# Branch B's key, value and query operands: split into halves at their source, and stored in DRAM as halves

## The chip, the cores and the metric

The kernel runs on one core of one Trainium2 chip. The metric is device time in microseconds (us) of one execution. A core has a matrix engine (TensorE, PE in the profile; its weight loads are shown as PEld), a vector engine (DVE), a scalar engine (ACT), GpSimd (POOL) and SyncE (SP). In this kernel SP issues every DMA; sixteen DMA engines carry them out.

## The reference

Two layers (DEPTH 2) of one mixer each run over 1024 latent tokens and 256 context tokens, 1280 in all, with D_MODEL 1024. Three branches work on the same normalised input: A is windowed grouped-query attention, B is multi-head latent attention, C is a gated convolution. Each branch is gated, projected and merged. Only branch B matters for the change. Cut to that:

```python
def mla_project(q_lat, kv_lat, g_qa, w_qb, g_kva, w_kvb):
    q = (rms_norm(q_lat, g_qa) @ w_qb).reshape(B, T, H_B, NOPE_B + ROPE_B)
    kv = (rms_norm(kv_lat, g_kva) @ w_kvb).reshape(B, T, H_B, NOPE_B + V_B)
    return q[..., :NOPE_B], q[..., NOPE_B:], kv[..., :NOPE_B], kv[..., NOPE_B:]

def block(qs):
    q_n, q_r = qs
    s = (jnp.einsum('bqhd,bkhd->bhqk', q_n, keys_n)
         + jnp.einsum('bqhd,bkd->bhqk', q_r, keys_r))
    p = jax.nn.softmax(s.astype(jnp.float32) * SCALE_B, axis=-1)
    return jnp.einsum('bhqk,bkhd->bqhd', p.astype(vals.dtype), vals)
```

There are 8 heads. `keys_n` is per head, `keys_r` (the rotary key) is shared by the heads. Latent queries read all 1280 keys; context queries read the 256 context keys, and are computed in layer 0 only, since the last layer's context output is not used.

## The kernel before

**Halves.** All matrix products are made in fp32r, a float32 that TensorE reads at its fast rate with fewer bits. To keep the accuracy, an operand x is split into a high half, hi = x rounded to fp32r, and a low half, lo = x - hi. `hi_act` (L104) makes hi on ACT, `lo_dve` (L110) makes lo on DVE. A product is then three passes, hi hi, hi lo and lo hi. In the profile the lines of these helpers, L105 and L111, stand for every split in the kernel; the tile's name tells which.

**Order of a layer.** `run` (L1594) goes through: input projection; token-major projections and branch C; then the preparation of the attentions: `a_prepare` (L892) and `b_keys` (L944), run alternately; `b_queries` (L1039); attention A (`attn_a`); attention B (`attn_b`, L1350) with branch A's merge as a filler; the second merge; the output projection.

**b_keys** writes three things to DRAM, as float32. The rotary key `krs` (64 rows by 1280 tokens) is transposed into PSUM, copied by DVE (L977) to a tile and stored. The keys `kns`, four tiles of 128 rows (two heads each), are projected by chunks of 512, 512 and 256 tokens, copied by DVE (L989) and stored. The values `vs`, ten tiles of 128 tokens by 512 columns, are projected, copied by ACT (L1005) and stored. The tiles share one ring of five 2 KB buffers, "kn". Between these steps `other()` runs one step of A's query preparation (tile "qq", ring of 4, stored to `qas`) or of the transposition of the q latents.

**b_queries** makes a head's queries chunk by chunk: nine matmuls, then one DVE multiplication by the rotation factors (L1054), then a store to `qs`. The factors are loaded for every head and chunk (L1046), although they depend only on the chunk and on whether the head is even. In layer 0 this is a stage of its own, 24 blocks. In layer 1 it has 16 blocks, which fill TensorE's gaps in attention A.

**attn_b** reads them back. Per head, `load_k` (three calls, one for each chunk) loads 64 rows of `kns` and 64 rows of `krs` into a staging tile and splits it into the K tile, `load_v` (two calls) does the same for V, and `load_q` for each unit of four query tiles. The staging tile has the tag "f", a ring of F_BUFS = 5 buffers, and the merge that runs beside it takes its own operands g and a from the same ring (L1472, L1473):

```python
f = stage()
nc.sync.dma_start(f[no : no + 64, :n], self.kns[h // 2][no : no + 64, o : o + n])
nc.sync.dma_start(f[ro : ro + 64, :n], self.krs[:, o : o + n])
halves(*(k_()[:, i, o : o + n] for i in range(2)), f[:, :n])
```

**Order inside attention.** `pipeline` (L1065) gives every piece of work (scores, maxima, exponentials, transposes, products with V, loads, filler) a due time on one axis, in estimated us of TensorE, and emits the pieces sorted by it. A unit is four query tiles of one head (and one of two context tiles in layer 0). A preparation of a unit is due at the unit's score start plus an offset: KP0 = -16 for the first K chunk and KP1 = 2 more for each further one, VP0 = 2 for V, QP0 = -5 for Q. K and V have two tiles each, Q three. Each engine runs its instructions in the order in which it got them, and SP issues its DMAs in order, waiting at each for its buffer.

## Time and profile before

| What | us |
| --- | --- |
| median of 3 runs | 3128.86 (3127.94 to 3136.29) |
| the profiled execution | 3132.84 |
| its span in the trace | 3131.1 |
| key preparation, layer 0 and layer 1 | about 925 to 969 and 2465 to 2504 |
| queries of B as a stage, layer 0 | about 969 to 1009 |
| attention A, layer 0 and layer 1 | about 1009 to 1212 and 2504 to 2665 |
| attention B, layer 0 and layer 1 | about 1209 to 1562 and 2664 to 2987 |

The times in the trace are us from the start of the span. The windows view gives, for a stretch, the busy time of each engine with its count of instructions, the clock that TensorE was granted (1.00 is full), the DMA engines' mean busy share and the GB/s that they moved. The view by lines gives for each group the busy time, the mean of one in ns, and the idle time of the engine just before it with what ended it.

### The profile page before, as it was taken

To read this page: it belongs to the slowest core of one execution; us is meant where nothing else is said; L and a number is where in the kernel's file an instruction comes from. 1 tells how busy PE (TensorE), PEld (TensorE's weight loads), DVE (VectorE), ACT (ScalarE), POOL (GpSimd) and SP (SyncE) were. 2 spreads that over 40 slices of the span, in tenths; PEclk is the share of its full clock that TensorE was granted. 3 is DMA by queue.
4 is the path that set the end of the run, shared out by engine and by line. 5 is a ranking of instruction groups with operands and counts; after the bars stand their busy time and mean duration, and the time that the engine had idled before them with its cause. 6 is when DMAs were issued, how large, how long until landed. Compare 5 with 4: busy or idle time off the path is not lost.

```text
span 3131.1 us, 54154 instructions
## 1 busy us (share of the span) xinstructions
PE 3001.9 (96%) x19731; PEld 2690.7 (86%) x19731; DVE 1879.6 (60%) x3213; ACT 1380.6 (44%) x3068; POOL 1413.2 (45%) x1809
## 2 busy tenths in 40 slices
PE   7899999989899999999999989999899999999998
PEld 4899999988897666777789889999889988778888
DVE  4744444444345766699854755555453577689863
ACT  3323333322222665478733423333322366568832
POOL 4545332332130666466652645444241367555641
PEclk9999999999999999999999989999999999999999
DMA  6122232245319434532063322333344442641153
GB/s 217 57 71 68 87 107 95 98 147 161 114 63 306 152 120 131 156 89 56 23 213 108 111 78 82 100 108 106 128 147 127 152 134 75 192 119 50 44 184 108
DMA packets 316227, 366.66 MB, mean 117 GB/s; under 512 B 51126, under 2 KB 242616, under 8 KB 315704
## 3 DMA queue, kind: packets, MB, share of 16 engines
q1 hardware_dynamic: 315960, 363.20, 36.3%
q8 instruction: 155, 2.54, 0.3%
q14 instruction: 112, 0.92, 0.1%
HBM read 256.02 MB, written 107.10 MB: 116 GB/s over the span
## 4 chain that ended last, share of the span: by engine, by line
PE 77%; DVE 7%; DMA 5%; issue 5%; ACT 4%; POOL 2%; SPq 0%; POOLq 0%; ACTq 0%; DVEq 0%
PE T L489 10%; PE T L488 10%; PE T L487 10%; PE T L115 8%; PE T L116 8%; PE T L117 8%; PE O L1198 6%; PE T L1185 5%; PE S L1414 4%; PE S L1283 2%; PE C L217 2%; ACT p L1160 1%; DVE ptL L111 1%; DVE tt L424 1%; DMA raw<-in_w_branch_dram 1%
## 5 line engine op out<-in xcount | busy, mean ns | idle before, releaser
L489 PE MATMUL T<-T,sl 128*128 128x320 f32 (+1 forms) x1408 | 416.5, 296 | 4.9 <-DVE sl L111 4.9
L115 PE MATMUL T<-wh,hm 128*128 128x288 f32 (+1 forms) x1328 | 385.7, 294 | 33.5 <-ACT wh L105 33.5
L487 PE MATMUL T<-T,sh 128*128 128x320 f32 (+1 forms) x1408 | 416.2, 296 | 0.6 <-ACT sh L105 0.6
L488 PE MATMUL T<-T,sh 128*128 128x320 f32 (+1 forms) x1408 | 416.1, 296 | 0.0
L116 PE MATMUL T<-wl,hm 128*128 128x288 f32 (+1 forms) x1328 | 387.2, 292 | 1.5 <-DVE wl L111 1.5
L117 PE MATMUL T<-wh,hm 128*128 128x288 f32 (+1 forms) x1328 | 388.6, 293 | 0.0
L111 DVE TENSOR_TENSOR ptL<-T,ptH 128x512 fp32r<-128x512 f32 (+2 forms) x512 | 335.3, 661 | 73.6 <-ACT ptH L105 70.1
L105 ACT ACTIVATE ptH<-T 128x512 fp32r<-128x512 f32 (+2 forms) x512 | 292.7, 577 | 155.6 <-PE T L1185 133.7
L487 PE MATMUL T<-hm,sh 128*128 128x320 f32 (+1 forms) x1056 | 313.4, 297 | 15.7 <-ACT sh L105 15.7
L493 DVE TENSOR_TENSOR px<-T,px 128x320 f32<-128x320 f32 (+1 forms) x440 | 194.9, 452 | 205.6 <-PE T L489 196.4
L489 PE MATMUL T<-hm,sl 128*128 128x320 f32 (+1 forms) x1056 | 313.0, 296 | 0.0
L488 PE MATMUL T<-hm,sh 128*128 128x320 f32 (+1 forms) x1056 | 312.9, 296 | 0.0
L1185 PE MATMUL T<-ident,p 128*128 128x128 f32 x1888 | 293.0, 275 | 13.0 <-DVE ptL L111 6.1
L1149 DVE TENSOR_REDUCE st<-S 128x1 f32<-128x1024 f32 (+2 forms) x288 | 269.9, 938 | 45.9 <-PE S L1414 19.0
L447 POOL TENSOR_TENSOR ssum<-sraw 128x512 f32<-128x512 f32 x88 | 114.5, 1301 | 395.3 <-DMA sraw<-in_w_in_dram 338.8
L1170 POOL TENSOR_SCALAR p<-p,st 128x1280 f32<-128x1280 f32 (+2 forms) x256 | 279.0, 1090 | 23.6
L115 PEld LDWEIGHTS T<-wh,hm 128*128 128x128 f32 x1328 | 254.2, 193 | 35.4 <-ACT wh L105 35.3
L1185 PEld LDWEIGHTS T<-ident,p 128*128 128x128 f32 x1888 | 221.9, 140 | 72.9 <-DVE ptL L111 21.5
L1160 ACT ACTIVATE p<-S,st 128x1024 f32<-128x1024 f32 (+2 forms) x256 | 241.0, 941 | 83.1 <-DVE st L1149 66.5
L489 PEld LDWEIGHTS T<-T,sl 128*128 128x128 f32 x1408 | 266.4, 189 | 5.4 <-DVE sl L111 5.4
L111 DVE TENSOR_TENSOR sl<-ssum,sh 128x512 fp32r<-128x512 f32 x176 | 163.6, 934 | 174.8 <-ACT sh L105 171.4
L487 PEld LDWEIGHTS T<-T,sh 128*128 128x128 f32 x1408 | 266.3, 189 | 0.8 <-ACT sh L105 0.8
(235 smaller groups left out, 7662.1 us busy)
## 6 DMA issues: line engine op xcount, KB each, us to landing
sraw<-in_w_in_dram SPq DMA_DIRECT2D x28, 1024.0 KB
wm<-in_w_mod_dram SPq DMA_DIRECT2D x24, 1024.0 KB
raw<-in_w_branch_dram SPq DMA_DIRECT2D x36, 512.0 KB
sraw<-in_w_in_dram SPq DMA_DIRECT2D x32, 512.0 KB
g<-sg SPq DMA_DIRECT2D x64, 256.0 KB
a<-macc SPq DMA_DIRECT2D x64, 256.0 KB
raw<-in_w_o_dram SPq DMA_DIRECT2D x14, 1024.0 KB
raw<-in_w_in_dram SPq DMA_DIRECT2D x10, 1024.0 KB
```

Source lines behind the costliest of these rows:

```text
L105: self.nc.scalar.activation(hi, src, AF.Copy)
L111: self.nc.vector.tensor_tensor(lo, src, hi.bitcast(F32), ALU.subtract)
L115: mm(out, lhsT=lh, rhs=rh, start=start, stop=False)
L116: mm(out, lhsT=lh, rhs=rl, start=False, stop=False)
L117: mm(out, lhsT=ll, rhs=rh, start=False, stop=stop)
L487: mm(out, lhsT=hi[:, k], rhs=tH, start=first and k == 0, stop=False, skip_group_check=True)
L488: mm(out, lhsT=hi[:, k], rhs=tL, start=False, stop=False, skip_group_check=True)
L489: mm(out, lhsT=lo[:, k], rhs=tH, start=False, stop=k == half - 1, skip_group_check=True)
L1149: nc.vector.reduce_max(st[:, 0:1], s, axis=AX.X, negate=True)
L1160: nc.scalar.activation(ptile(o, o + ap.shape[-1]), ap, AF.Exp, bias=st[:, len(parts) - 1 : len(parts)], accum_out=st[:, 2 + i : 3 + i])
L1170: nc.gpsimd.tensor_scalar(p, p, st[:, 4:5], 1.0, op0=ALU.mult, op1=ALU.mult)
L1185: nc.tensor.transpose(pt[:, w : w + P], blk, self.ident)
```

## The change

- `b_keys` splits at the source: a new helper `send` takes a result from PSUM, makes hi on ACT and lo on DVE side by side in one tile, and stores both with one DMA. The values are treated alike. The ring "kn" has three buffers of twice the size; the ring "qq" has three for four.
- `krs`, `kns`, `vs` and `qs` in DRAM get a dimension of two for the halves.
- `b_queries` loads the factors once for each chunk and head parity, and runs the chunks in the outer loop and the heads in the inner one. In layer 0 (`self.nq == NT`) it splits the queries and stores two halves; in layer 1 it stores them whole, in the first half.
- `attn_b` loads K as one piece and V as one piece, halves and all, straight into their tiles; in layer 0 also Q. In layer 1 Q is still split there. KP1 is gone, VP0 is 0.

```diff
-KP0, KP1, VP0, QP0 = -16.0, 2.0, 2.0, -5.0
+KP0, VP0, QP0 = -16.0, 0.0, -5.0
...
+        def both():
+            return kp.tile([P, 2, 512], F32R, tag="kn", name=self.nm("kn"), bufs=3)
+
+        def send(dst, rows, o, n, pt):
+            x = both()[:rows, :, :n]
+            self.hi_act(x[:, 0], pt[:rows, :n])
+            self.lo_dve(x[:, 1], pt[:rows, :n], x[:, 0])
+            nc.sync.dma_start(dst[:, :, o : o + n].rearrange("i p t -> p i t"), x.bitcast(F32))
...
-            kr = kp.tile([P, 512], F32, tag="kn", name=self.nm("kr"), bufs=5)
-            nc.vector.tensor_copy(kr[:64, :n], pt[:64, :n])
-            nc.sync.dma_start(self.krs[:, o : o + n], kr[:64, :n])
+            send(self.krs, 64, o, n, pt)
...
-                kn = kp.tile([P, 512], F32, tag="kn", name=self.nm("kn"), bufs=5)
-                nc.vector.tensor_copy(kn[:, :n], pt)
-                nc.sync.dma_start(self.kns[p][:, o : o + n], kn[:, :n])
+                send(self.kns[p], P, o, n, pt)
...
-            vv = kp.tile([P, H * HD], F32, tag="kn", name=self.nm("vv"), bufs=5)
-            nc.scalar.activation(vv, pt, AF.Copy)
-            nc.sync.dma_start(self.vs[:, t], vv)
+            vv = both()
+            self.hi_act(vv[:, 0], pt)
+            self.lo_dve(vv[:, 1], pt, vv[:, 0])
+            nc.sync.dma_start(self.vs[:, t], vv.bitcast(F32))
...
-            nc.sync.dma_start(self.qs[h][:, o : o + n], q[:, :n])
+            if self.nq < NT:
+                nc.sync.dma_start(self.qs[h][0, :, o : o + n], q[:, :n])
+                return
+            hi, lo = (pool.tile([P, 512], F32R, tag=f"qo{i}", name=self.nm("qo"), bufs=3) for i in "HL")
+            self.hi_act(hi[:, :n], q[:, :n])
+            self.lo_dve(lo[:, :n], q[:, :n], hi[:, :n])
+            for i, x in enumerate((hi, lo)):
+                nc.sync.dma_start(self.qs[h][i, :, o : o + n], x[:, :n].bitcast(F32))
...
-        for h in range(H):
-            for c in self.chunks:
-                got = self.lazy(lambda h=h, c=c: load(h, c))
+        for c in self.chunks:
+            tabs = [self.lazy(lambda e=e, c=c: load(e, c)) for e in range(2)]
+            for h in range(H):
+                got = tabs[h % 2]
...
+            def load_k(h=h, no=no, ro=ro, k_=k_):
+                for r, src in ((no, self.kns[h // 2][:, no : no + 64]), (ro, self.krs)):
+                    nc.sync.dma_start(k_()[r : r + 64].bitcast(F32), src.rearrange("i p t -> p i t"))
+
+            def load_v(h=h, v_=v_):
+                for i in range(2):
+                    nc.sync.dma_start(
+                        v_()[:, :, i * HD : (i + 1) * HD].bitcast(F32), self.vs[:, :, i, h * HD : (h + 1) * HD]
+                    )
...
+                if self.nq == NT:
+                    nc.sync.dma_start(q_()[:, :, :n].bitcast(F32), src.rearrange("i p t -> p i t"))
+                    return
...
+            kprep = [(KP0, load_k), (VP0, load_v)]
```

The ring of the factors' tile goes from 6 to 4 buffers in layer 0 and from 2 to 3 in layer 1.

More of the change, by code (lines that the diff above doesn't have):

```diff
@@ L918, in step @@
             for i, (a, b) in enumerate(((0, 64), (64, 0))):
-                q = tp.tile([P, 512], F32R, tag="qq", name=self.nm("qq"), bufs=4)
+                q = tp.tile([P, 512], F32R, tag="qq", name=self.nm("qq"), bufs=3)
                 self.hi_act(q[a : a + 64, :n], pt[a : a + 64, :n])
@@ L1041, in b_queries, with load @@
         nc = self.nc
-        def load(h, c):
+        def load(e, c):
             o, n = CH[c]
             tb = pool.tile([P, 512], F32, tag="tab", name=self.nm("tab"), bufs=bufs)
-            nc.sync.dma_start(tb[:, :n], self.a["k_rope_t"][h % 2][:, o : o + n])
+            nc.sync.dma_start(tb[:, :n], self.a["k_rope_t"][e][:, o : o + n])
             return tb
@@ L1367, in attn_b @@
             v_ = self.lazy(lambda: tp.tile([P, NT, P], F32R, tag="v", name=self.nm("v"), bufs=2))
-            def load_k(c, h=h, no=no, ro=ro, k_=k_):
-                o, n = CH[c]
-                f = stage()
-                nc.sync.dma_start(f[no : no + 64, :n], self.kns[h // 2][no : no + 64, o : o + n])
-                nc.sync.dma_start(f[ro : ro + 64, :n], self.krs[:, o : o + n])
-                halves(*(k_()[:, i, o : o + n] for i in range(2)), f[:, :n])
-            def load_v(c, h=h, v_=v_):
-                t0, nt = c * (NT // 2), NT // 2
-                f = stage()[:, : nt * HD].rearrange("p (t d) -> p t d", d=HD)
-                nc.sync.dma_start(f, self.vs[:, t0 : t0 + nt, h * HD : (h + 1) * HD])
-                halves(*(v_()[:, t0 : t0 + nt, i * HD : (i + 1) * HD] for i in range(2)), f)
+            def load_k(h=h, no=no, ro=ro, k_=k_):
[6 more added lines that the diff above has]
+                    )
             def load_q(q_, t0, t1, h=h):
                 n = (t1 - t0) * P
+                src = self.qs[h][:, :, t0 * P : t1 * P]
+                if self.nq == NT:
+                    nc.sync.dma_start(q_()[:, :, :n].bitcast(F32), src.rearrange("i p t -> p i t"))
+                    return
                 f = stage()
-                nc.sync.dma_start(f[:, :n], self.qs[h][:, t0 * P : t1 * P])
+                nc.sync.dma_start(f[:, :n], src[0])
                 halves(*(q_()[:, i, :n] for i in range(2)), f[:, :n])
-            kprep = [(KP0 + i * KP1, lambda c=c, load_k=load_k: load_k(c)) for i, c in enumerate((0, 1, 2))]
-            kprep += [(VP0 + c * KP1, lambda c=c, load_v=load_v: load_v(c)) for c in range(2)]
+            kprep = [(KP0, load_k), (VP0, load_v)]
             def score(t, t0, q, k_=k_):
@@ L1665, in run @@
             self.bz = [self.dram([P, T], F32, "bz") for _ in range(4)]
-            self.krs = self.dram([64, T], F32, "krs")
-            self.kns = [self.dram([P, T], F32, "kns") for _ in range(4)]
+            self.krs = self.dram([2, 64, T], F32, "krs")
+            self.kns = [self.dram([2, P, T], F32, "kns") for _ in range(4)]
             self.qas = [self.dram([P, T], F32, "qas") for _ in range(H)]
-            self.qs = [self.dram([P, T], F32, "qs") for _ in range(H)]
+            self.qs = [self.dram([2, P, T], F32, "qs") for _ in range(H)]
             self.vas = self.dram([P, NT, 4 * HD], F32, "vas")
-            self.vs = self.dram([P, NT, H * HD], F32, "vs")
+            self.vs = self.dram([P, NT, 2, H * HD], F32, "vs")
             self.in_proj(ew, first, begin, ehp.close)
@@ L1694, in run @@
                 qp = self.pool(el, "qp")
-                steps = self.b_queries(qp, ws, qH, qL, self.bank, 6)
+                steps = self.b_queries(qp, ws, qH, qL, self.bank, 4)
                 for i, (_, _, fn) in enumerate(steps):
@@ L1709, in run @@
             if last:
-                fill = self.b_queries(lp, ws, qH, qL, self.cbank, 2)
+                fill = self.b_queries(lp, ws, qH, qL, self.cbank, 3)
             else:
```

## The prediction

> **What bounds the kernel now.** I read the page's table of engines, then the windows over the stages that the change touches, then lines and timelines inside them. The page first:
>
> ```profile
> span 3131.1 us, 54154 instructions
> PE 3001.9 (96%) x19731; PEld 2690.7 (86%) x19731; DVE 1879.6 (60%) x3213; ACT 1380.6 (44%) x3068; POOL 1413.2 (45%) x1809
> ```
>
> TensorE (PE) is busy 96% of the span, so an edit that takes work from DVE and ACT only pays where one of these makes PE late. The windows (PE, PEld, DVE, ACT, POOL busy, clock, DMA share, GB/s) of the steady part of attention B, a stretch and three heads of layer 0, then three stretches of layer 1:
>
> ```profile
> 1346.00:1378.22 32.22, 29.68 (x169) 22.87 (x169) 31.50 (x55) 26.26 (x62) 22.35 (x29) 1.00 0.40 112
> 1413.40:1449.94 36.54, 35.43 (x206) 28.80 (x207) 33.95 (x60) 30.87 (x70) 28.05 (x38) 1.00 0.23 63
> 1449.94:1485.26 35.32, 34.73 (x206) 28.87 (x206) 32.43 (x60) 30.63 (x70) 19.29 (x29) 1.00 0.18 50
> 1485.26:1521.50 36.24, 35.40 (x206) 28.82 (x206) 34.02 (x60) 30.78 (x70) 27.99 (x38) 1.00 0.15 43
> 2780.00:2800.00 20.00, 19.11 (x110) 15.12 (x109) 19.79 (x35) 16.97 (x38) 15.06 (x18) 1.00 0.45 129
> 2851.36:2883.94 32.58, 32.54 (x193) 27.15 (x193) 30.64 (x54) 28.12 (x62) 22.65 (x31) 1.00 0.23 64
> 2916.20:2948.00 31.80, 31.78 (x187) 26.23 (x186) 28.18 (x49) 25.84 (x56) 22.60 (x30) 1.00 0.12 35
> ```
>
> DVE is nearly full in all of them, and in layer 0 PE has holes beside it (29.68 of 32.22 us in the first row). A head of layer 0 takes 36.0 us (mean of rows two to four); one of layer 1 takes 32.6 us (the 2851 row) with PE closed. So DVE limits layer 0's heads, PE those of layer 1.
>
> The windows of the key preparation and the query projection tell another story:
>
> ```profile
> 925.00:1009.00 84.00, 83.70 (x462) 70.16 (x461) 53.23 (x101) 31.37 (x71) 3.05 (x6) 1.00 0.86 290
> 933.00:941.00 8.00, 8.00 (x52) 6.91 (x51) 7.69 (x18) 2.98 (x6) 0.00 (x0) 1.00 0.63 216
> 957.00:965.00 8.00, 8.00 (x44) 6.50 (x43) 3.73 (x8) 5.63 (x12) 0.00 (x0) 1.00 1.03 375
> 973.00:981.00 8.00, 8.00 (x41) 6.68 (x40) 3.20 (x7) 0.00 (x0) 0.00 (x0) 1.00 1.02 356
> 2465.00:2507.00 42.00, 41.30 (x239) 34.60 (x237) 33.21 (x63) 26.12 (x60) 4.08 (x8) 1.00 0.81 283
> 2497.00:2505.00 8.00, 8.00 (x36) 6.44 (x35) 0.71 (x2) 3.95 (x8) 0.00 (x0) 1.00 0.95 352
> ```
>
> Here PE is closed and the DMA engines are almost full too: a share of 0.86 in layer 0, 0.81 in layer 1, with 375 GB/s the most that a full stretch moved. This is where the change doubles what is written.
>
> **Part 1: the splits leave attention B.** By lines and forms, DVE in layer 0's attention B (1209 to 1562 us), and then in layer 1's (2664 to 2987 us):
>
> ```profile
> L111 DVE TENSOR_TENSOR k<-f,k 128x512 fp32r<-128x512 f32 x16 | 14.3, 898 | 3.9 <-ACT k L105 3.7
> L111 DVE TENSOR_TENSOR q<-f,q 128x512 fp32r<-128x512 f32 x16 | 13.6, 852 | 2.9 <-ACT q L105 2.9
> L111 DVE TENSOR_TENSOR v<-f,v 128x320 fp32r<-128x320 f32 x16 | 10.7, 666 | 0.0
> L111 DVE TENSOR_TENSOR k<-f,k 128x256 fp32r<-128x256 f32 x8 | 4.2, 526 | 6.7 <-ACT k L105 6.7
> L111 DVE TENSOR_TENSOR q<-f,q 128x256 fp32r<-128x256 f32 x8 | 4.1, 508 | 1.0 <-ACT q L105 1.0
> ```
>
> ```profile
> L111 DVE TENSOR_TENSOR k<-f,k 128x512 fp32r<-128x512 f32 x16 | 11.0, 708 | 3.1 <-ACT k L105 3.1
> L111 DVE TENSOR_TENSOR v<-f,v 128x320 fp32r<-128x320 f32 x16 | 10.9, 704 | 0.4 <-ACT v L105 0.4
> L111 DVE TENSOR_TENSOR k<-f,k 128x256 fp32r<-128x256 f32 x8 | 4.6, 569 | 2.4 <-ACT k L105 2.4
> ```
>
> Layer 0 loses 14.3 + 13.6 + 10.7 + 4.2 + 4.1 = 46.9 us of DVE, 5.9 us a head. Layer 1 keeps the split of Q (its queries are still written whole) and loses 26.5 us. What is that worth? In layer 0 a head's DVE falls from 33.5 (mean of the three rows) to 27.6 us, and PE is late next. PE's own need I take from layer 1: 32.6 us, plus the context unit, which layer 1 does not have: per head 10 matmuls of 256 columns and 4 transposes. Their spacing stands in PE's timeline, the 256-column starts 0.12 us apart and ten transposes in 1.26 us:
>
> ```profile
> 1236.11 0.28 PE L116 MATMUL T<-yL,wh 128*128 128x256 f32 x1
> 1236.23 0.28 PE L117 MATMUL T<-yH,wl 128*128 128x256 f32 x1
> ...
> 924.79 1.26 PE L905 MATMUL T<-ident,kA 128*128 128x128 f32 x10
> ```
>
> That is 10 x 0.12 + 4 x 0.11 = 1.6, so 34.2 us a head: 1.8 us saved on each of about five heads (1378 to 1562 us), **-9**. The bounds are 0 (the holes are PE's own order) and -14 (also the DVE-full 1346 row, and every head at 33.5). Layer 1 gives nothing in the steady part: from 2916.20 no next head is split, and PE still needs 31.80/187 = 0.170 us per matmul, against 32.58/193 = 0.169. Only 2780 to 2820 us, where DVE is full while the merge ends, can give its idle time, 0.9 us of the row and about as much behind it: **-1.5**.
>
> **Part 2: the start of attention B.** The staging tile "f" has five buffers, shared with the merge's g and a. SP's timeline and PE's show what that does in layer 0:
>
> ```profile
> 1211.23 0.59 SPq L1373 DMA_DIRECT2D f<-krs  x1
> 1219.90 0.44 SPq L1372 DMA_DIRECT2D f<-kns  x1
> ```
>
> ```profile
> 1223.26 0.96 PE L1414 MATMUL C<-k,q 128*128 128x256 f32 x3 [1.36 <-ACT k L105]
> 1226.43 0.50 PE L115 MATMUL T<-yH,wh 128*128 128x512 f32 x1 [1.51 <-DVE g L1481]
> ```
>
> SP stands 8.7 us before K's third chunk because no buffer is free, and the merge's next g queues behind it. With K and V landing in their own tiles the merge has the five buffers alone. Two stalls of 2.87 us can go, and the later ones of this kind with them; against that K's first load now has to land whole, 2 x 5120 B x 128 rows = 1.31 MB (3.5 us at the 375 GB/s of the 957 row; the SP row issues one chunk of it 12 us ahead of PE's stall), and V's load comes earlier in the queue. I take **-3** here and **-2** in layer 1, between 0 and -5 each. Part 1 and 2 sum to -15.5; the bounds are -3 and -25.
>
> Two new waits I cost at nothing. K's load on SP now waits itself for the K tile of two heads before; by the planner's times it is issued just after that head's last score, some 16 us of the planner ahead of its need, and what stands behind it on SP (z, the next Q, the merge's loads) is due later still. It frees SP too: two issues for K a head in place of six, at the 0.44 to 0.59 us of the rows above. And the queries, now computed by chunk and then by head, still lie in DRAM before attention B asks for the first: in layer 1 all of them run inside attention A. Both would cost a merge stall such as the 1.51 us above if I have the order wrong.
>
> **Part 3: preparation.** The page's DMA issues (both layers; KB each):
>
> ```profile
> tab<-in_k_rope_t_dram SPq DMA_DIRECT2D x32, 256.0 KB
> qs<-qo SPq DMA_DIRECT2D x32, 256.0 KB
> vs<-vv SPq DMA_DIRECT2D x20, 256.0 KB
> kns<-kn SPq DMA_DIRECT2D x16, 256.0 KB
> kns<-kn SPq DMA_DIRECT2D x8, 128.0 KB
> krs<-kr SPq DMA_DIRECT2D x4, 128.0 KB
> ```
>
> Per layer vs adds 10 x 256 KB, kns 8 x 256 + 4 x 128 KB, krs 320 KB by its tiles' sizes: 5440 KB = 5.57 MB. In layer 0 qs adds its own 5120 KB again, and the factors fall from 24 loads to 6, from 5120 to 1280 KB; net 1.31 MB more. Layer 0's stage moved 84 us x 290 GB/s = 24.4 MB and will move 31.2; layer 1's moved 42 x 283 = 11.9 and will move 17.5. At 375 GB/s these take 83 and 47 us; at the rate of the stages per full share (290/0.86 = 337, 283/0.81 = 349) 93 and 50 us. So layer 0 grows by 0 to 9 us, layer 1 by 5 to 8, and a ring with less in flight (kn 3 for 5, qq 3 for 4) can lose some 3 us more in each. I take **+6** and **+7**: nearer the slow rate, since early in the stage DVE is full and DMA is not (the 933 row: 7.69 of 8 us, a share of 0.63), and these bytes cannot be moved ahead. It is not hidden: attention A's first load of Q is queued on SP behind all these writes. The Trainium skill, "DMA: Bandwidth & Descriptors", Specifications, gives about 358 GB/s as what the HBM yields one core; the 375 GB/s row is above it. With its figure the two stages would take an estimated 87 and 49 us, 3 and 7 us more than now, for which the loss would be 10 in place of 13 us.
>
> By lines and forms, the copy that goes and what stands in its place:
>
> ```profile
> L989 DVE COPY kn<-T 128x512 f32<-128x512 f32 x16 | 11.0, 690 | 0.4
> L111 DVE TENSOR_TENSOR ptL<-T,ptH 128x512 fp32r<-128x512 f32 x448 | 304.8, 686 | 59.7 <-ACT ptH L105 56.7
> L105 ACT ACTIVATE ptH<-T 128x512 fp32r<-128x512 f32 x448 | 265.5, 597 | 121.0 <-PE T L1185 106.8 <-PE O L1198 9.3 <-DVE st L1149 0.5
> ```
>
> The engines' share lies inside that. Kn's and kr's copies on DVE become subtractions of the same shape at no cost: a copy took 690 ns, a subtraction from PSUM 686. ACT gains their high halves, 15 x at most 0.60 us, where it is busy 2.98 of 8 us (the 933 row). V's eviction gains a subtraction, 10 x 0.69 us on DVE, in a section where DVE is idle 4.3 of 8 us in layer 0 (the 957 row) and 7.3 of 8 in layer 1. The query stage's new ACT and DVE work (24 blocks, at most 0.60 and 0.85 us) lies where ACT is at 0.00 and DVE at 3.20 of 8 us (the 973 row). Behind each such wait stand the evictions that free PSUM, so what DMA holds up reaches PE after eight banks.
>
> **Sum.** -9 - 1.5 - 3 - 2 + 6 + 7 = -2.5 us, on a profiled run of 3132.84 us (span 3131.1). The runs shown have a median 4.0 us below that run, so the forecast for the median is 3128.86 - 2.5 = **3126.4**. About 0.3% (9.4 us) is what a measurement here can tell from no change.
>
> **The rivals.**
> - *The preparation hides its writes* (0.31): rings and eight PSUM banks carry them while layer 0's query stage, rid of 18 factor loads, catches up. For it: 375 and 356 GB/s are reached in whole windows, and PE does not fall below 8.00 of 8 beside them. Against it: the share is at 0.86 on average already. Then the loss is 3 and not 13: -12.5, **3116**.
> - *The writes decide, slower* (0.22): the stages run at 337 and 349 GB/s with the ring loss, 9 + 3 and 8 + 3, so +23, and attention B gives 11 of its 15.5: +12, **3141**. It decides as soon as the DMA rate over the two stages stays under about 330 GB/s. For it: the early window is at 216 GB/s with DVE full, and ACT and DVE must now take turns on each K chunk.
> - *The splits were never late* (0.07): PE's order makes layer 0's holes, so Parts 1 and 2 give 5, the preparation costs 10: +5, **3134**, within 0.3%. Against it: DVE at 31.50 of 32.22 us beside a PE with 2.5 us of holes.
>
> **How the numbers follow.** The forecast has 0.40. Faster by over 0.3% (below 3119.5): the first rival and a little of the forecast, 0.33. Slower by over 0.3% (above 3138.2): most of the second rival, 0.20. Within: 0.47. The range leaves out a tenth on each side, beyond both rivals' points: 3108 to 3143; the likeliest case's own range is 3117 to 3135.
>
> **What would show it.** Right: heads of layer 0's attention B at about 34 us with DVE near 28; no SP gap before K's load at the start of attention B; the stage from the kr transposes to attention A's first score longer by about 6 and 7 us at a DMA share above 0.9. Wrong: heads still at 36 us with DVE free (third rival); stages as long as now (first rival); or a DMA share below 0.9 with PE waiting on evictions, which would put the loss on the rings or on ACT and DVE taking turns, and not on bandwidth.

## The result, and the profile after

The change is slower: 3164.3 us median of 4 runs (3162.1 to 3169.45) against 3128.4 of 4 runs of the kernel before on the same chip; ratio 1.0111, 95% interval 1.0096 to 1.0127. That is about 35 us, and outside the predicted range. The profiled execution took 3169.45 us, its span 3167.7 us; before it was 3131.1.

The page of the changed kernel, its engines (busy us, share of the span, instructions):

```profile
span 3167.7 us, 53895 instructions
PE 3008.8 (95%) x19731; PEld 2696.7 (85%) x19731; DVE 1840.5 (58%) x3153; ACT 1364.7 (43%) x3018; POOL 1396.5 (44%) x1809
```

DVE lost 39 us of work, as meant, and TensorE did as many matmuls as before. Its busy time grew by 6.9 us, so 29.7 of the 36.6 us of span are time in which TensorE had nothing. To find it I cut both traces at the same instructions: the first transpose of kr, the first and the last multiply of a query block (DVE), the first score of attention A, the first score of attention B, and attention B's last product with V. In us:

| stretch | before | after | difference |
|---|---|---|---|
| L0, kr to first query multiply (K, V) | 45.8 | 58.3 | +12.5 |
| L0, first to last query multiply | 36.6 | 39.0 | +2.4 |
| L0, last query multiply to attention A | 7.1 | 17.8 | +10.7 |
| L0, attention A | 204.3 | 208.7 | +4.4 |
| L0, attention B | 353.2 | 342.2 | -11.0 |
| between the layers' stages | 893.0 | 892.8 | -0.2 |
| L1, kr to attention A | 44.9 | 56.9 | +12.0 |
| L1, attention A | 161.1 | 168.5 | +7.4 |
| L1, attention B | 314.5 | 312.7 | -1.8 |

Attention B of L0 gained about what was forecast for it (11.0 of 12). The preparations lost 37.6 us, where 13 were forecast, and attention A became longer in both layers. Windows of the changed kernel (us, then PE, PEld, DVE, ACT, POOL busy, clock, DMA share, GB/s): the whole preparation of L0, four stretches in it, then the start and the end of L1's:

```profile
926.10:1041.20 115.10, 92.74 (x469) 72.24 (x467) 73.22 (x137) 54.12 (x112) 2.69 (x5) 0.90 0.86 304
960.00:968.00 8.00, 8.00 (x41) 6.41 (x40) 6.18 (x12) 5.59 (x12) 0.00 (x0) 1.00 1.01 388
976.00:984.00 8.00, 1.81 (x8) 1.13 (x6) 1.11 (x2) 0.38 (x1) 0.24 (x1) 0.85 1.03 358
1021.00:1029.00 8.00, 2.20 (x20) 1.92 (x18) 3.52 (x10) 1.67 (x4) 0.00 (x0) 0.81 0.79 254
1029.00:1037.00 8.00, 1.28 (x4) 0.39 (x5) 1.29 (x2) 2.43 (x3) 0.00 (x0) 0.50 1.02 329
2485.00:2493.00 8.00, 7.75 (x53) 6.50 (x52) 7.64 (x16) 7.76 (x22) 1.38 (x4) 1.00 0.75 225
...
2525.00:2533.00 8.00, 0.15 (x1) 0.00 (x0) 3.61 (x6) 2.98 (x5) 0.00 (x0) 0.68 0.91 361
```

Where TensorE was full before, it now has three holes. TensorE's timeline names what ended them (start, duration, instruction; in brackets the idle time before it and its releaser):

```profile
986.67 0.79 PE L115 MATMUL T<-qTH,wh 128*128 128x512 f32 x1 [8.86 <-ACT wh L105]
...
1035.72 5.53 PE L217 MATMUL C<-wm,sc 128*2 128x256 f32 x16 [11.74 <-DMA wm<-in_w_mod_dram]
...
2533.25 0.79 PE L115 MATMUL C<-qTH,wh 128*128 128x512 f32 x1 [8.10 <-DVE kn L111]
```

The first is the wait for the second half of the query weights: its load is now the last thing on SP behind all of V's stores and those of attention A's queries, and with the blocks ordered by chunk it is needed after 4 of them, not 12. The third, in L1, ends with an eviction of V (tile kn); the section on K and V comes back to it. The second is the wait for wm, the first weight of the modulation, a filler of attention A that comes ahead of its first score. SP's timeline of the changed kernel shows where that load stands, and the one of the kernel before where it stood:

```profile
1009.71 16.07 SPq L1068 DMA_DIRECT2D qs<-qo  x24
...
1027.40 0.38 SPq L208 DMA_DIRECT2D wm<-in_w_mod_dram  x1
...
1031.46 1.83 SPq L1275 DMA_DIRECT2D q<-qas  x2
```

```profile
996.16 0.46 SPq L208 DMA_DIRECT2D wm<-in_w_mod_dram  x1
...
1009.54 0.32 SPq L1261 DMA_DIRECT2D q<-qas  x1
```

Before, wm went out among the query stores, 12 us ahead of the last query multiply (1008.3). Now it follows all 48 of them. The instruction streams say why: there it waited for a free DMA slot alone, here for four DMAs. The query pool grew from 20 to 28 kB a partition (tiles qoH and qoL), and attention A's first tiles now lie on memory from which query stores are still read: in both programs wm's first tile starts at byte 117,920 of a partition and the query pool at 96,416, so that the pool ended at 116,896 and now ends at 125,088.

### The profile page after: what moved, and what is told of

The parts are those of the page before. It is cut to its first block, busy times and chain, and to the rows that moved or that the text cites. A ratio compares the mean times of both kernels' runs of the same rounds, so it can differ in the third digit from the quotient of the medians.

```text
span 3167.7 us, 53895 instructions
## 1 busy us (share of the span) xinstructions
PE 3008.8 (95%) x19731; PEld 2696.7 (85%) x19731; DVE 1840.5 (58%) x3153; ACT 1364.7 (43%) x3018; POOL 1396.5 (44%) x1809
## 4 chain that ended last, share of the span: by engine, by line
PE 81%; DVE 6%; DMA 6%; ACT 3%; issue 2%; POOL 2%; SPq 0%; ACTq 0%; POOLq 0%; DVEq 0%
PE T L489 10%; PE T L487 10%; PE T L488 10%; PE T L115 9%; PE T L116 8%; PE T L117 8%; PE O L1212 6%; PE T L1199 6%; PE S L1428 5%; PE S L1297 2%; PE C L217 2%; PE C L1428 1%; DMA wm<-in_w_mod_dram 1%; DMA raw<-in_w_branch_dram 1%; DVE tt L424 1%
## 5 line engine op out<-in xcount | busy, mean ns | idle before, releaser
L487 PE MATMUL T<-hm,sh 128*128 128x320 f32 (+1 forms) x1056 | 313.7, 297 | 15.6 <-ACT sh L105 15.6
L115 PEld LDWEIGHTS T<-wh,hm 128*128 128x128 f32 x1328 | 254.9, 193 | 36.6 <-ACT wh L105 36.5
L487 PEld LDWEIGHTS T<-T,sh 128*128 128x128 f32 x1408 | 265.8, 189 | 0.4 <-ACT sh L105 0.4
L488 PEld LDWEIGHTS T<-T,sh 128*128 128x128 f32 x1408 | 265.9, 189 | 0.0
```

What stands on the lines that cost most here:

```text
L115: mm(out, lhsT=lh, rhs=rh, start=start, stop=False)
L487: mm(out, lhsT=hi[:, k], rhs=tH, start=first and k == 0, stop=False, skip_group_check=True)
L488: mm(out, lhsT=hi[:, k], rhs=tL, start=False, stop=False, skip_group_check=True)
```

## The experiments

Three theories. **Bandwidth**: the doubled stores fill the DMA engines. **Order**: the change puts loads behind stores, by the order of blocks or by the memory overlap. **Rings**: three tiles for five (kn) and for four (qq) hold the evictions up. All 18 runs in one table, in us by the cuts above; "K, V" is kr to the first query multiply, "queries" from there to attention A's first score. The ratio is to the kernel before on the same chip, since that kernel's median lay between 3128 and 3141 us from one chip to the next. The stretches come from one profiled execution each. The one between the layers, which no version touches, came to 888 to 893 us in them, so a difference of 2 or 3 us in a single long stretch says little.

| run | L0 K, V | L0 queries | L0 att. A | L0 att. B | L1 prep. | ratio (95%) |
|---|---|---|---|---|---|---|
| before | 45.8 | 43.7 | 204.3 | 353.2 | 44.9 | 1 |
| the change | 58.3 | 56.8 | 208.7 | 342.2 | 56.9 | 1.0111 (1.0096 to 1.0127) |
| half_order | 58.8 | 56.7 | 207.3 | 343.3 | 58.2 | 1.0108 (1.0089 to 1.0127) |
| b_rings | 47.2 | 42.8 | 207.2 | 354.0 | 44.1 | 1.0016 (1.0005 to 1.0028) |
| halfwrite | 47.5 | 55.9 | 207.6 | 341.6 | 44.2 | 1.0021 (1.0009 to 1.0034) |
| qwhole | 59.5 | 41.6 | 207.0 | 347.0 | 58.9 | 1.0069 (1.0051 to 1.0088) |
| qp20 | 59.2 | 49.2 | 214.1 | 341.2 | 58.4 | 1.0104 (1.0087 to 1.0120) |
| b_double | 57.2 | 43.4 | 205.3 | 353.0 | 55.8 | 1.0082 (1.0067 to 1.0097) |
| b_qhalf20 | 45.9 | 52.3 | 206.8 | 348.0 | 45.5 | 1.0049 (1.0032 to 1.0066) |
| vpacked | 58.2 | 56.7 | 207.7 | 342.0 | 57.8 | 1.0110 (1.0095 to 1.0125) |
| factors | 46.1 | 39.9 | 206.9 | 354.9 | 46.7 | 1.0000 (0.9988 to 1.0013) |
| factors_half | 45.9 | 40.0 | 210.8 | 357.4 | 45.5 | 1.0008 (0.9999 to 1.0016) |
| v_pool | 46.0 | 43.2 | 204.3 | 350.5 | 45.7 | 0.9999 (0.9989 to 1.0009) |
| fh_vpool | 46.2 | 39.8 | 208.2 | 349.3 | 45.4 | 1.0006 (0.9995 to 1.0016) |
| qhigh | 59.1 | 55.1 | 207.1 | 343.8 | 58.3 | 1.0099 (1.0081 to 1.0116) |
| b_qdouble | 46.0 | 54.7 | 206.8 | 352.9 | 45.5 | 1.0041 (1.0026 to 1.0055) |
| l0_vpool | 46.3 | 43.3 | 204.2 | 350.6 | 45.6 | 0.9990 (0.9978 to 1.0002) |
| l0_vqpool | 45.8 | 43.1 | 204.2 | 355.7 | 45.3 | 1.0003 (0.9992 to 1.0014) |
| qhigh20 | 59.1 | 48.8 | 207.6 | 343.4 | 58.8 | 1.0089 (1.0067 to 1.0112) |
| b_pool28 | 46.4 | 51.5 | 206.8 | 353.4 | 45.6 | 1.0027 (1.0010 to 1.0044) |

### K and V: the bytes decide

**halfwrite** stores only the high halves of kr, k and v (attention B loads them twice); **b_double** adds the bytes alone to the kernel before; **b_rings** the short rings alone.

```diff
# halfwrite, on the change (k and kr alike)
-nc.sync.dma_start(self.vs[:, t], vv.bitcast(F32))
+nc.sync.dma_start(self.vs[:, t, 0], vv[:, 0].bitcast(F32))
# b_double, on the kernel before (k and kr alike)
 nc.sync.dma_start(self.vs[:, t], vv)
+nc.sync.dma_start(self.vs2[:, t], vv)
# b_rings, on the kernel before (kr and vv alike)
-name=self.nm("kn"), bufs=5)
+name=self.nm("kn"), bufs=3)
-name=self.nm("qq"), bufs=4)
+name=self.nm("qq"), bufs=3)
```

> The change, but only the high halves of kr, k and v are stored; attention B loads the high half twice in place of high and low, so the loads stay as many and as large. The output is therefore not the reference's. The stores of the keys' and values' stages are back at the bytes of before; the query stores of L0 stay doubled, rings and order as in the change. Theory 'bandwidth': the stage of L1 from its first kr transpose to attention A's first score (44.0 us before, 55.9 after) goes back to 44 to 47 us, that of L0 (89.5 and 115.1 us) to 103 to 108, time 3140 to 3148. Theory 'late loads': the PE wait of 8.9 us in L0 stays, L1 gains at most 3 us, 3157 to 3164. Theory 'rings': a tile comes free sooner because its store is half as long, so nearly as under 'bandwidth' in L1 (45 to 49 us).

> The kernel before, with each store of kr, k and v issued a second time to a spare place in DRAM, in both layers: 5.57 MB more a layer, with the engines' work, the rings (five and four tiles), the order and the queries as before. Theory 'bandwidth': L1's stage from kr to attention A's first score goes from 44.9 to 54 to 58 us as in the change (56.9), L0's from 89.5 to 97 to 104, time 3146 to 3156. Theory 'rings and order': with five tiles and the old order the bytes are hidden at least by half: L1 45 to 50, L0 90 to 94, time 3128 to 3138.

> The kernel before, with the two rings that the change shortens made as short: three tiles instead of five for kr, kn and vv, three instead of four for qq. Nothing is stored twice and nothing is reordered. Theory 'rings': the waits on vs<-kn come back, the keys' and values' stages of L0 and L1 grow by 4 to 10 us each, 3136 to 3148. Theories 'late loads' and 'bandwidth': the shorter rings cost little while the stores are short, 3126 to 3132.

Without the low halves' stores, and with every tile still split by ACT and DVE in rings of three, the K and V stretch of L0 is back at 47.5 us and L1's preparation at 44.2. With five tiles, the old order and unsplit tiles, the second stores alone bring 57.2 and 55.8. Short rings alone bring 47.2 and 44.1. So the bytes decide, and the short rings cost nothing here by themselves. Windows of L1's preparation, halfwrite first, then b_double with its last three stretches:

```profile
2470.00:2514.20 44.20, 40.40 (x231) 33.72 (x229) 39.98 (x76) 33.99 (x73) 3.19 (x7) 1.00 0.82 290
```

```profile
2477.50:2533.30 55.80, 42.17 (x235) 34.89 (x232) 32.05 (x60) 24.68 (x53) 3.15 (x7) 0.90 0.94 339
2509.00:2517.00 8.00, 8.00 (x36) 6.44 (x35) 1.38 (x2) 3.25 (x6) 0.00 (x0) 1.00 1.03 379
2517.00:2525.00 8.00, 1.44 (x7) 0.76 (x5) 0.00 (x0) 1.79 (x3) 0.00 (x0) 0.79 1.03 382
2525.00:2533.00 8.00, 1.18 (x3) 0.86 (x4) 0.91 (x2) 0.77 (x3) 1.70 (x3) 0.50 1.01 354
```

In b_double TensorE runs out of work at 2518 us while the DMA engines stay full for another 15. What it lacks is in the waits of DVE in that run (total us, times, longest):

```profile
DVE qo L1057 <- DMA tab<-in_k_rope_t_dram: 19.7, 1, 19.7
```

DVE stood that long for one load of 256 kB, the first rotation factors, issued behind the stores that were still going out; TensorE stood behind the full PSUM banks. In L1 of the change itself the engines stand at another place for the same stores. ACT waits for a free tile of the ring of three before it can evict V, and DVE then waits 5.9 us for the first factors (ACT's waits from 2515 to 2541 us):

```profile
ACT kn L105 <- DMA vs<-kn: 6.7, 7, 1.9
```

With the ring of five and no splits b_double loses nearly as much (57.2 and 55.8 us against 58.3 and 56.9), so ring and splits together add about 1 us a layer to the bytes. What is shown is the cost of these bytes in the order that the kernel has: no run issues the first factor load ahead of V's stores, so it is open how much of them could go out under attention A, where the DMA share is 0.29 to 0.37. In the total, K's and V's bytes make 0.82% (b_double) to 0.90% (1.0111 less halfwrite's 1.0021), 26 to 28 us of the change's 35. b_rings was slower in total, by 0.05 to 0.28%; its stages show 2.9 and 3.5 us more in the two attentions A, which I can't explain.

### Queries of L0: not the bytes, not the hole

**half_order** runs heads 0 to 3 over all chunks, then 4 to 7. **qwhole** stores the queries whole. **qhigh** stores only their high halves.

```diff
# half_order, on the change
-for c in self.chunks:
+for c, g in [(c, g) for g in (0, 4) for c in self.chunks]:
...
-    for h in range(H):
+    for h in range(g, g + 4):
# qwhole, on the change (and f staged and split again in attention B)
-if self.nq < NT:
+if True:
     nc.sync.dma_start(self.qs[h][0, :, o : o + n], q[:, :n])
     return
# qhigh, on the change
-for i, x in enumerate((hi, lo)):
-    nc.sync.dma_start(self.qs[h][i, :, o : o + n], x[:, :n].bitcast(F32))
+nc.sync.dma_start(self.qs[h][0, :, o : o + n], hi[:, :n].bitcast(F32))
```

> The change, with its query blocks in another order: heads 0 to 3 over all chunks, then heads 4 to 7 over all chunks, the factors loaded once per chunk and half. The bytes stored, the rings and the number of query stores stay; only the second half of the query weights is needed after 12 blocks (8 in L1) and not after 4. Theory 'late loads' (the change orders work so that a load is asked for later than it is needed): the PE wait of 8.9 us at 987 us in L0 is gone or under 2 us, attention A's first score of L0 moves from 1041.2 to 1028 to 1033 us, and the time from 3164 to 3150 to 3156. Theory 'bandwidth' (the doubled stores decide): the same bytes, so first score within 3 us of 1041 and 3161 to 3167. Theory 'rings' (three kn tiles and three qq tiles instead of five and four hold the evictions up): the same rings, 3161 to 3167.

> The change without its query part: in L0 too the queries are stored whole and split in attention B; the stores and loads of k and v, the rings and the chunk-major order stay. 24 query stores instead of 48 in L0. Theory 'late loads': the wait of 8.9 us stays, but the weights and the query that attention A starts with are issued some 4 to 8 us sooner after the last query block, first score of L0 at 1030 to 1035 us instead of 1041.2; attention B of L0 pays some of its splits again (342 us becomes 343 to 350); 3156 to 3164. Theory 'bandwidth': 5 MB less to store at 350 GB/s are 15 us in L0, first score at 1025 to 1028, 3150 to 3156.

> The change, but of L0's queries only the high halves are stored, and attention B loads them twice in place of high and low; the output is therefore not the reference's. The low halves are still computed, the pool of 28 kB, the rings, the chunk-major order and attention A's loads behind the last query store stay; 5.24 MB less are stored. From the first query block to attention A's first score the change takes 56.8 us, the kernel before 43.7, the run without the query part (qwhole) 41.5. Theory 'bytes': 42 to 46 us, total 3148 to 3154. Theory 'order and memory': 51 to 57 us, total 3158 to 3165.

half_order took the first hole away, and nothing was won: 56.7 us. TensorE's timeline of half_order, all its waits of over 1 us from the first query block on:

```profile
996.51 0.39 PE L115 MATMUL T<-qTH,wh 128*128 128x256 f32 x1 [1.81 <-DVE qo L1060]
1025.05 0.16 PE L1292 MATMUL S<-sink,ones 128*128 128x1 bf16 x1 [3.48 <-DVE qo L1060]
1028.98 0.16 PE L1292 MATMUL S<-sink,ones 128*128 128x1 bf16 x1 [3.77 <-DVE qo L1060]
1043.46 5.25 PE L217 MATMUL C<-wm,sc 128*2 128x256 f32 x16 [14.31 <-DMA wm<-in_w_mod_dram]
```

The 8.9 us came back as a longer wait for wm and two for the query evictions: the hole was not on the path that sets the end. qwhole gave 41.6 us, less than before the change; so the query part is what costs. But qhigh, with 5.24 MB less to store and all else kept, still took 55.1. Windows of qhigh, query stage and what follows:

```profile
1007.00:1015.00 8.00, 8.00 (x36) 6.44 (x35) 5.12 (x8) 2.45 (x4) 0.00 (x0) 1.00 0.35 131
1015.00:1023.00 8.00, 8.00 (x59) 7.44 (x58) 6.11 (x13) 3.60 (x8) 0.00 (x0) 1.00 0.38 138
1023.00:1031.00 8.00, 3.49 (x31) 3.21 (x29) 5.56 (x13) 4.24 (x9) 0.00 (x0) 0.85 0.68 223
1031.00:1039.00 8.00, 1.50 (x4) 0.47 (x5) 0.00 (x0) 0.24 (x1) 0.00 (x0) 0.50 0.93 303
```

The DMA engines are little more than a third busy while TensorE computes queries, and busy at a share of 0.93 when it has nothing: wm and attention A's loads only then go out. My bandwidth theory falls for this stretch.

### The memory overlap

**b_pool28** puts the overlap alone into the kernel before; **qp20** and **qhigh20** take it out of the change and of qhigh, at the price of two tiles for each of qo, qoH and qoL; **b_qdouble** adds query stores to the kernel before.

```diff
# b_pool28, on the kernel before
-name=self.nm("qo"), bufs=4)
+name=self.nm("qo"), bufs=(4 if self.nq < NT else 8))
# qp20 and qhigh20, on the change and on qhigh
-name=self.nm("qo"), bufs=4)
+name=self.nm("qo"), bufs=(4 if self.nq < NT else 2))
-name=self.nm("qo"), bufs=3)
+name=self.nm("qo"), bufs=2)
# b_qdouble, on the kernel before
 nc.sync.dma_start(self.qs[h][:, o : o + n], q[:, :n])
+if self.nq == NT:
+    nc.sync.dma_start(self.qs2[h][:, o : o + n], q[:, :n])
```

> The kernel before with eight qo tiles in L0 in place of four: the query pool grows from 20 to 28 kB, and nothing else changes; attention A's first weight loads now stand behind the last query store. Theory 'memory': from the first query block to attention A's first score 49 to 55 us instead of 43.7, total 3133 to 3140. Rival 'engines and rings': 42 to 45 us, total 3127 to 3131.

> The change with two tiles each for qo, qoH and qoL in L0 in place of four, three and three: the query pool takes 20 kB a partition as before the change, not 28. Same bytes, same order of blocks. In the change attention A's first tiles overlap the larger query pool in SBUF, so their loads are issued behind the last query store. Theory 'memory' (that overlap is what makes attention A's loads late): the first weight load of attention A is issued among the query stores again, the PE wait of 11.7 us on it at 1035 us is under 3 us, the stage from kr's first transpose to attention A's first score takes 103 to 109 us instead of 115.1, and the time is 3152 to 3159. Theory 'bandwidth' (stores fill the DMA engines, so an earlier load only pushes stores back): 112 to 118 us, 3160 to 3167; the shorter rings may even cost a little.

> qhigh (only the high halves of L0's queries stored; the output is not the reference's) with two tiles each of qo, qoH and qoL, so that the query pool is 20 kB and attention A's first loads may go out among the query stores. Theory 'memory' (their place behind the last store costs the time): from the first query block to attention A's first score 41 to 46 us (55.1 in qhigh), attention A as long as there (207), total 3150 to 3157. Rival 'engines and rings' (ACT and DVE work on the halves, short rings): 51 to 57, total 3160 to 3168.

> The kernel before, with each query store of L0 issued a second time to a spare place: 5.24 MB more, all 24 factor loads, order, pool and engines' work as before, K and V whole. From the first query block to attention A's first score before: 43.7 us. Theory 'bytes': 5.24 MB at 340 GB/s are 15 us, 54 to 60 us, total 3139 to 3146. Theory 'order and memory': 44 to 50 us, total 3128 to 3135.

b_pool28 computes and stores what the kernel before does, in the same order of blocks, with eight tiles of qo for four. It lost 7.8 us in the query stretch, at one place of TensorE's timeline; SP's timeline shows the load behind the last store, some 15 us later than before:

```profile
1020.35 5.03 PE L217 MATMUL C<-wm,sc 128*2 128x256 f32 x16 [9.86 <-DMA wm<-in_w_mod_dram]
```

```profile
1010.39 0.40 SPq L1055 DMA_DIRECT2D qs<-qo  x1
...
1012.19 0.46 SPq L208 DMA_DIRECT2D wm<-in_w_mod_dram  x1
```

So the overlap alone costs about 8 us. The other runs fit: in all six kernels with the pool of 28 kB (the change, half_order, halfwrite, vpacked, qhigh, b_pool28) the first load of wm follows the last query store, and TensorE waits 9.9 to 14.3 us for it; of the fourteen with 16 or 20 kB only b_qdouble has that order. Taking the overlap out does not give them back where the rings must pay: qp20 gained 7.6 us in the query stretch and lost 5.4 in attention A, with no difference in the total that can be told. DVE's waits in qp20 say where it went:

```profile
DVE qo L111 <- DMA qs<-qo: 14.8, 9, 4.0
```

Two tiles are too few when two stores go out for each block. qhigh20 came to 48.8 us, 6.3 under qhigh, above the 41 to 46 that 'memory' alone expected; DVE there waits 11.0 us for ACT's halves. Near the end of the stretch TensorE waits 5.3 us in qp20 and 5.1 in qhigh20 for a DVE eviction of queries (L1060), in qwhole for none. So of the query part's 15.2 us (56.8 against qwhole's 41.6) about 8 are the overlap, and the rest I can place only roughly, with the halves' evictions and their rings. b_qdouble lost 11.0 us and seemed to speak for bytes; but wm stands behind the last store there too (TensorE waits 7.9 us for it), though its pool has 20 kB and the tiles do not overlap. Why it stands there is open, and the run tells nothing apart.

### Attention B, and versions that might have won

**b_qhalf20** and **factors** are the query part and the factor part alone; **factors_half** orders by halves of the heads as well. **v_pool**, **l0_vpool** and **l0_vqpool** take low halves of V (and Q) in attention B from DVE to POOL, in both layers or in L0 alone; **fh_vpool** is factors_half with v_pool. **vpacked** lays V's halves of a head side by side.

```diff
# factors, on the kernel before (factors_half: the loop of half_order)
-for h in range(H):
-    for c in self.chunks:
-        got = self.lazy(lambda h=h, c=c: load(h, c))
+for c in self.chunks:
+    tabs = [self.lazy(lambda e=e, c=c: load(e, c)) for e in range(2)]
+    for h in range(H):
+        got = tabs[h % 2]
# v_pool, on the kernel before, in load_v, written out (l0_vpool: in L0; l0_vqpool: in load_q as well)
-self.lo_dve(lo, f, hi)
+nc.gpsimd.tensor_tensor(lo, f, hi.bitcast(F32), ALU.subtract)
# vpacked, on the change (the stores alike)
-for i in range(2):
-    nc.sync.dma_start(
-        v_()[:, :, i * HD : (i + 1) * HD].bitcast(F32), self.vs[:, :, i, h * HD : (h + 1) * HD]
-    )
+nc.sync.dma_start(v_().bitcast(F32), self.vs[:, :, h * 2 * HD : (h + 1) * 2 * HD])
```

> The kernel before with the query part of the change alone: in L0 the queries go through DRAM as halves and are not split in attention B, factors loaded once per chunk for heads 0 to 3 and again for 4 to 7, two tiles each of qo, qoH and qoL so that the pool stays at 20 kB. K and V as before. Net 2.6 MB more in L0, none in L1. Attention B of L0 saves DVE 17.7 us of splits; in the change Q's part of the gain was 347.0 - 342.2 = 4.8 us. Theory 'bandwidth': 2.6 MB at 330 GB/s are 8 us, of which the stage's slack hides some: L0's stage 92 to 98 us instead of 89.5, attention B 347 to 350, total 3126 to 3134. Theory 'memory and order': with the overlap and the late weights gone the stores are hidden, L0's stage 89 to 92, total 3121 to 3127.

> The kernel before with the factor part of the change alone: query blocks by chunk and then by head, each factor chunk loaded once (6 loads in L0 for 24, 4 in L1 for 16). No halves in DRAM. 3.84 MB less in L0. Theory 'bandwidth': L0's stage from kr to attention A's first score (89.5 us before) is closed on TensorE, so fewer bytes give little: 86 to 90 us, total 3123 to 3130. Theory 'order': the second half of the query weights, now needed after 4 blocks and loaded behind the stores of the stage, opens a PE hole of 3 to 9 us by itself: 92 to 98 us, total 3131 to 3139.

> As the run before, with heads 0 to 3 over all chunks first and then 4 to 7, so that the second half of the weights is needed after 12 blocks as before the change; 12 factor loads in L0 for 24, 2.56 MB less. Theory 'bandwidth': 86 to 90 us, total 3122 to 3130, no difference that can be told from none, or up to 4 us faster. Theory 'order': the same, since no hole is left; so the pair of runs gives the hole's price as their difference, 0 to 2 us under 'bandwidth', 4 to 9 under 'order'.

> The kernel before, with the low halves of V in attention B subtracted on GpSimd (POOL) and not on VectorE (DVE): 16 x 0.67 us leave DVE in each layer, and no byte in DRAM is added. It asks whether splits that leave DVE are worth in attention B of L0 what the change got for them, 0.23 us of span for each us of DVE (10.9 for 46.9). If DVE sets the pace of L0's heads: attention B of L0 350 to 352 us instead of 353.2, total 1 to 4 us faster, 3125 to 3128. Rival: POOL is late instead (its merge work in the first heads, 28 of 36 us busy), or the heads wait for something else: 353 to 357, total 3129 to 3135.

> The kernel before, with the low halves of V subtracted on POOL in L0's attention B alone: 10.7 us leave DVE. If DVE sets the pace of L0's heads: attention B of L0 349 to 352 us (353.2 before; 350.5 and 349.3 in the two runs with V on POOL in both layers), L1 unchanged, total 1 to 4 us faster. Rival: POOL's later work pays it back, 352 to 356, total within 2 us.

> As the run before, with the low halves of Q on POOL as well in L0: 28.4 us leave DVE, some 45 us go to POOL, which is busy 25 of 36 us a head. At 0.23 us for each us of DVE, as the change got: attention B of L0 345 to 349 us, total 4 to 8 us faster than before. Rival: Q's low half comes later from POOL (about 1.3 us for 0.85) and the scores wait for it: 352 to 360, total 0 to 6 us slower.

> The kernel before with factors loaded once per chunk and half (no hole) and V's low halves on POOL: the two parts that cost no DRAM byte, together. If both hold, L0's stage 86 to 90 us, attention B 350 to 352: 3120 to 3127, faster than both kernels. If neither does, 3129 to 3135.

> The change with V's halves of a head side by side in DRAM, so that attention B's load of V takes rows of 512 bytes in one load and not rows of 256 bytes in two; the bytes are the same. In the change the DMA engines were full at only 204 to 243 GB/s where attention B of L1 starts. Theory 'small rows' (V's load holds up K's, the merge's and the next loads there): the starts of attention B gain 1 to 4 us each, 3156 to 3162. Rival: K's first load is late by itself and V's is hidden: 3162 to 3167.

The factor part alone opens no hole: the query weights come late only when K's and V's doubled stores are ahead of them. It shortens the query stretch by 3.8 us, attention A and B are 2.6 and 1.7 us longer, and the total stays. Of the two parts of the gain in attention B, K's and V's came to 353.2 - 347.0 = 6.2 us (qwhole) and the queries' to 4.8 to 5.2 (347.0 - 342.2, and b_qhalf20). V's subtractions moved to POOL in L0 gave 2.6 us there for 10.7 us of DVE, 0.24 us for each, the price that the whole change got (11.0 for 46.9); with Q's too, attention B was longer than before. Windows of attention B of L0, l0_vpool, then l0_vqpool:

```profile
1225.20:1575.80 350.60, 333.18 (x1900) 269.27 (x1899) 281.41 (x483) 247.81 (x556) 222.55 (x295) 1.00 0.34 101
```

```profile
1222.10:1577.80 355.70, 334.39 (x1900) 269.71 (x1899) 265.84 (x460) 246.89 (x556) 245.43 (x318) 1.00 0.34 99
```

DVE's busy time fell by 15.6 us more in the second and the stretch grew by 5. TensorE's waits for POOL in it rose from 0.7 to 4.4 us (1.8 for Q's halves, 2.6 for p): taking work from DVE pays only while the engine that takes it over delivers as early. No version is shown to beat the kernel before; l0_vpool's interval, 0.9978 to 1.0002, still holds no change.

vpacked raised what the full DMA engines move at the start of L1's attention B. Two windows of the change there, then the same of vpacked:

```profile
2702.00:2710.00 8.00, 3.24 (x14) 2.28 (x13) 0.69 (x1) 0.63 (x1) 1.46 (x2) 0.92 1.04 243
2710.00:2718.00 8.00, 7.73 (x26) 6.40 (x27) 4.12 (x7) 1.68 (x5) 2.16 (x4) 0.65 1.02 204
```

```profile
2702.00:2710.00 8.00, 5.57 (x25) 4.24 (x24) 1.99 (x2) 0.63 (x1) 3.43 (x4) 1.00 1.04 257
2710.00:2718.00 8.00, 8.00 (x38) 6.33 (x39) 5.13 (x8) 3.32 (x8) 3.79 (x6) 1.00 1.10 255
```

With V in rows of 512 bytes in place of 256 the second window moved 255 GB/s against 204 at a full share, and the first wait for K fell from 5.03 to 2.43 us. The total didn't follow: 1.0110. The Trainium skill, "DMA: Bandwidth & Descriptors", Specifications, asks for at least 512 bytes a transfer for line rate; the two windows agree in direction. The loads around V's are the same ones, though not at the same moments.

## Why the prediction was wrong

**Part 3, the preparation, is where most of it failed**: +6 and +7 us were forecast, 25.6 (115.1 - 89.5) and 12.0 came. Two steps of it failed, in different ways. The rest of the miss lies in Parts 1 and 2: the attentions were to give 15.5 us and gave about 1 in this pair of profiles.

*The size of K's and V's bytes, in both layers.* The mechanism was right, the term was mis-sized: b_double puts it at 11.1 and 10.9 us. In L1 I took 42 us at 283 GB/s, 11.9 MB, and let 17.5 MB run at 349 to 375 GB/s. But the stage that counts ends with attention A's first score, 44.9 us and 12.8 MB. That stage before, and then in the change:

```profile
2465.90:2510.80 44.90, 42.64 (x241) 35.36 (x238) 33.79 (x66) 26.62 (x57) 3.18 (x7) 1.00 0.81 286
```

```profile
2484.90:2541.80 56.90, 45.67 (x239) 36.47 (x238) 39.09 (x72) 32.61 (x70) 3.18 (x7) 0.91 0.91 331
```

b_double moved 55.8 x 339 = 18.9 MB, at a share of 0.94. A rate "per full share" and a best window were used as if the stage could hold them from end to end; its first 8 us ran at 225 GB/s in the change, since the stores only begin there, and what is not moved early must be waited for late. And "eight banks" were not cover enough: the factor load stood behind all the stores. The figure of the Trainium skill that I weighed ("DMA: Bandwidth & Descriptors", Specifications, about 358 GB/s for one core) would have given an estimated 7 us for L1 and been low too; the 960 window of the change reached 388.

*The query stage of L0.* I counted "net 1.31 MB more" and stopped at bytes. The stretch grew by 13 us for other reasons: about 8 are the larger query pool (b_pool28), and what is left lies, as far as the runs tell, with the work on the halves. That the pool's size decides when the next phase's loads may start was in none of my steps; I wrote that attention A's first load of Q is queued behind all these writes, and didn't see that wm, which had gone out early, would join it. Nor do saved and stored bytes offset each other: the factor part alone gave 3.8 us, and the query part with half of its stores left out (qhigh) was 1.7 us shorter than with all.

*The rings*, "some 3 us more in each", cost nothing by themselves in these stages (b_rings), and with the splits about 1 us beside the doubled bytes. *The engines' share* "lies inside" was right for K and V: halfwrite splits everything and is within 2 us of before. For the queries it was not: without the overlap and with before's bytes, qhigh20 still took 48.8 us against qwhole's 41.6.

**Part 1, near in attention B's sum, and not in place.** -12 was forecast for L0 with Part 2, 11.0 came in attention B. Heads were to take 34.2 us with DVE near 28. Four heads of the changed kernel:

```profile
1400.92:1435.77 34.85, 34.63 (x208) 28.67 (x207) 28.59 (x52) 27.08 (x62) 18.63 (x29) 1.00 0.40 95
1435.77:1471.10 35.33, 35.11 (x208) 28.64 (x207) 28.96 (x52) 27.19 (x62) 26.47 (x38) 1.00 0.46 113
1471.10:1506.02 34.92, 34.70 (x208) 28.67 (x207) 28.59 (x52) 27.06 (x62) 18.66 (x29) 1.00 0.41 95
1506.02:1541.30 35.28, 35.05 (x208) 28.72 (x207) 28.90 (x52) 27.08 (x62) 26.45 (x38) 1.00 0.46 113
```

DVE is at 28.8, PE is closed as foreseen, but at 35.1 us a head: PE's own need was put 0.9 too low. The prediction's three rows already had PE busy for 35.2 of 36.0 us a head, so that DVE could hardly be worth 1.8. Compared with like heads of before (POOL busy for 28 or for 19 us) these gave 1.1 or 0.4 us each, about 3 in all, and about half of the gain lies ahead of them, where attention B shares its engines with the merge. The sums of six windows of 30 us from attention B's first score, before and then after:

```profile
sum 180.00, PE 167.89 PEld 135.35 DVE 136.44 ACT 108.36 POOL 104.59; mean PE 27.98 PEld 22.56 DVE 22.74 ACT 18.06 POOL 17.43
```

```profile
sum 180.00, PE 173.28 PEld 143.09 DVE 123.28 ACT 100.78 POOL 102.93; mean PE 28.88 PEld 23.85 DVE 20.55 ACT 16.80 POOL 17.15
```

TensorE got 5.4 us more into the same 180. L1's -1.5 can't be told: attention A and B of L1 together took 475.6 us before and 481.2 in the change, but 474.1 to 480.4 in all runs that keep K and V whole and 474.1 to 481.2 in all that store halves of them.

**Part 2, the start of attention B, failed.** -5 was forecast. The gap before K's third chunk went, but the load of K "now has to land whole", and that was priced at 3.5 us with some 12 us of lead. In L1 of the change it went out at 2697 us, and the first score could start at 2710, 13 us later. TensorE's timeline of the change shows it waiting for that, and then for the merge's g, in L0 and in L1:

```profile
1249.95 1.62 PE L1428 MATMUL S<-k,q 128*128 128x512 f32 x6 [1.75 <-DMA k<-krs]
1267.32 0.58 PE L115 MATMUL T<-yH,wh 128*128 128x256 f32 x1 [5.67 <-DVE g L1495]
...
2710.27 2.90 PE L1428 MATMUL S<-k,q 128*128 128x512 f32 x6 [5.03 <-DMA k<-krs]
2726.96 0.79 PE L115 MATMUL T<-yH,wh 128*128 128x512 f32 x1 [4.09 <-DVE g L1495]
```

In the first 100 us or so of the stage TensorE's waits for K and for g went from 4.7 to 7.4 us in L0 and from 0.8 to 9.1 in L1. The wait for K ends at the first score of attention B, so the cuts count it in attention A: it is 1.75 of A's 4.4 us more in L0 and 5.03 of its 7.4 in L1. In L1 a wait of 1.5 us for a query eviction adds to it; what is left, 2.7 us in L0, I can't place. Why the merge's g came later no run shows; with V in one load (vpacked) its first long wait in L1 was 2.16 us.

"Two new waits I cost at nothing": the one for the tile two heads back indeed cost nothing that the waits show; the queries' new order made the hole of 8.9 us, which half_order shows to cost nothing by itself here.

**The rivals.** "The writes decide, slower" had the bytes and its condition: the rates were 304 and 331 GB/s, about 313 over both stages. Its ring loss did not show, and its price, +23 for both stages, was 15 us short, by the query pool and again by the rates. The prediction's sign for a loss on rings, a share below 0.9, came in L0 (0.86), but there TensorE waits for the query weights and for wm, and not for evictions. "The preparation hides its writes" and "the splits were never late" are refuted, by b_double and by attention B's 342 us.

## What to carry to other kernels

That the DMA share of a stage is below 1 does not make more bytes free: here the share was 0.8, 5.57 MB more cost 11 us in each layer, and the first load queued behind them is what the engines wait for, so price the landing of that load, at the rate of the whole stage. When a change enlarges a pool, look which later tiles will lie on its memory: their loads move behind the last use of it, at once and without any line of code for it. And a hole that shows in the timeline is worth what its removal moves the end, which only a run tells.

## What the hardware showed that I had not expected

After a hole TensorE restarts slowly. In b_double's timeline, behind its longest hole:

```profile
2531.82 0.79 PE L115 MATMUL C<-qTH,wh 128*128 128x512 f32 x1 [10.60 <-DVE qo L1057]
2532.41 0.63 PE L116 MATMUL C<-qTL,wh 128*128 128x512 f32 x1
2532.84 0.63 PE L117 MATMUL C<-qTH,wl 128*128 128x512 f32 x1
```

The same matmul took 0.39 us before the hole, and the granted clock of that window was 0.50. The Trainium skill, "TensorE: Matmul & The Clock Gate", Part 1, says that the array's clock is halved once it has been idle for a window of about 3.4 us and is full again only after as long of steady work; the rows agree on the half, and 3.7 us after the restart, at 2535.51, the same matmul takes 0.39 us again. Two of the changed kernel's holes end with the same 0.79 us (986.67 and 2533.25), so they cost a little more than their length.
